# Retention's queries and keys through a DRAM scratch, two changed waiting rules and float32 norm sums in a two-layer hybrid encoder

## The chip, the cores and the metric

One core of a Trainium2 chip runs the whole program. The metric is the device time of one execution in microseconds (us). Engines are named as the profile names them: PE (TensorE matmuls), PEld (its weight loads), DVE (VectorE), ACT (ScalarE), POOL (GpSimd) and SP (SyncE), whose queue (SPq) issues nearly all of the transfers here.

## The reference

Two layers on a (1, 512, 1024) float32 input. What is computed in each:

```
x = x + 0.5 * SwiGLU(RMSNorm(x))                       # d_ff 2816
h = RMSNorm(x);  P = h @ W_in                          # A, B, C heads and three gates
A: 4 heads of differential attention: q, k of two maps each, normed and rotated,
   block-causal mask, softmax(s0) - lam * softmax(s1), values of 128, RMS norm per head
B: 8 heads of chunked attention, q and k normed, a relative-position bias, values of 64
C: 4 heads of retention: q and k rotated, scores times a decay, values of 128,
   RMS norm per head, times silu(g)
x = x + (sum_i sigmoid(g_i) * (branch_i @ W_branch_i)) @ W_out
x = x + 0.5 * SwiGLU(RMSNorm(x))
```

The kernel computes retention as one masked 512 x 512 product per head instead of a recurrence over chunks; the decay table holds zero above the diagonal.

## The kernel before

**Arithmetic.** Float32 accuracy is made of fp32r matmuls. Each operand is split into a high and a low part (ACT copies the high part, DVE subtracts: `xh`/`xl`, `wh`/`wl`, `yh`/`yl`, `qh`/`ql`), and a product takes three matmuls: high·high, high·low, low·high. Activations lie with features on the partitions, in tiles of 128 x 512 from a ring of 72 buffers (`big`). A weight tile of 128 x 1024 (`wr`) is loaded by SP into one of three raw buffers and split into `wh` and `wl`; 24 matmuls of 512 columns use one such tile in a projection.

**Stages of a layer.** An FFN, the mixer, an FFN. The mixer projects A's q, k, v, then B's, then the gates of branch 0 and C's gate `g` (four projections), multiplies A's result by its branch weights (`branch(0)`), projects C's q, k and v, then `branch(1)` for B and `branch(2)` for C. Each `branch` first computes eight gate projections from the normed input `xn` and then eight output tiles from the split results `ys` of that mixer, twelve matmuls each, `yh` and `yl` of four tiles.

**Heads between the projections.** Attention and retention run as side programs (Python generators), stepped between the matmuls of the projections. After every projection matmul `tick` may run the next piece of one of them. All instructions of an engine run in the order in which this planner emits them, so its order is fixed when the kernel is built. A small cost model (`Model`) keeps a clock per engine and a time for each tile; a piece is let in when PE's clock has passed the ready time of the tiles named in its last `yield` plus a margin: `then` none, `room` 800 ns, `product` 1600 ns, `turn` 2400 ns, and 1500 ns for the norm totals. A transfer counts as landed 2500 ns after its issue (`sent`). Two heads, one preparation and up to two finishing programs are active at a time.

**A head's end.** `settle_head` squares the head's output, splits the square and sums it over partitions with two matmuls against a matrix of ones (the total: `bank<-yh,ones`, then `bank<-yl,ones`). ACT copies half of the result to `ss`. When both heads of a pair are done, `finish` makes r = 1/sqrt on DVE (12 operations, `v`, `r`, `n`), SP scatters r to the two `rh` tiles with four transfers, and per head DVE multiplies `yu` by gain and `rh` (and for C by the gate `cs`), ACT makes `yh`, DVE `yl`.

**Stacked tiles.** The scores use tiles in which a head's 64 rows stand beside their other part, so that two matmuls do the work of three: for q the high over the low part, for k one tile of the high part twice and one of the low part twice (`qk`). [...] For A and B a tile takes two transfers of 64 rows (`twice`). For C the rows of a head come in two halves of 32 from two tiles (`rotated` gives rows 0 to 31 of all four heads in one tile and rows 32 to 63 in the other), so that a tile takes four transfers of 32 rows (L1003 to L1022). Per mixer these are 16 transfers for q and 32 for k, all on the SP queue, on which the weight loads stand too.

**The norm totals.** `norm_rows` sums the squares of x over the features. DVE or POOL adds the squares of the eight tiles into `acc`; then `acc` is split and summed with two fp32r matmuls against the ones. It serves the FFNs (L454, L479) and, through `norm_tokens`, the mixer.

The functions that the diff touches follow with their line numbers.

Of the kernel before, what the change touches and what calls it, by code (L numbers as in the profile page):

```python
# [11 lines left out]
F32 = mybir.dt.float32  # L12
# [7 lines left out]
S = 512  # L20
# [31 lines left out]
class Model:  # L52
# [29 lines left out]
        end, by = max(self.read.get(self.key(ap), [(0.0, "pe")]))  # L82
        self.slots[self.owner.pop(self.key(ap))] = end + self.LAG[by]

    def sent(self, ap, wait=2500):

        self.wrote[self.key(ap)] = max(self.t.values()) + wait, "pe"

# [34 lines left out]
def then(*aps):  # L123

    return aps, False, 0
# [7 lines left out]
def room(*aps):  # L133

    return aps, True, Kernel.MARGIN


def turn(*aps):

    return aps, True, Kernel.TURN  # L140


class Kernel:
# [254 lines left out]
            nc.scalar.activation(out=sq, in_=x, func=AF.Square)  # L398
            eng.tensor_tensor(out=self.acc, in0=self.acc, in1=sq, op=ALU.add)

    def norm_rows(self):

        parts = yield from self.split_side(self.acc)
        yield parts[1:], True, self.NORM
        b = self.bank()
        self.total(b, parts)
        self.rb = self.pool.tile([P, S], F32, tag="rb", bufs=2, name=self.name("rb"))
        yield then(b)
        yield from self.rsqrt_wide(self.rb, b, 1.0 / D, EPS)
# [40 lines left out]
    def opening_norm(self):  # L450
        for k in range(KD):
            self.norm_square(k, self.nc.vector)
            yield room(self.acc)
        yield from self.norm_rows()  # L454

    def ffn(self, l, gnext, late=1):
        nc = self.nc
        xs = self.xn
        ps = []

        def hidden():
            bg, bu = held.pop(0)
            t = self.big(F32, "t")
            nc.vector.tensor_tensor(out=t, in0=bg, in1=self.rb, op=ALU.mult)
            self.free(bg)
            nc.scalar.activation(out=t, in_=t, func=AF.Silu)
            nc.vector.tensor_tensor(out=t, in0=t, in1=bu, op=ALU.mult)
            self.free(bu)
            ps.append(self.split2(t, "p"))

        held = []
        for f in range(NF):
            if self.opening:
                held.append(self.open(xs))
                self.prio.append([0, self.opening_norm(), "n", None, True])
                continue
            bg = self.proj(xs)
            if f == 0:
                self.prio.append([0, self.norm_rows(), "n", None, True])  # L479
                self.step(self.prio)  # L480
            if f >= late:
                self.settle()
                if len(held) > 1:
                    hidden()
            held.append((bg, self.proj(xs)))
            if f >= late:
                hidden()
        while held:
            hidden()
        rb = self.rb  # L490
        self.xn = []
        wt = None
        at = 8
        for m in range(KD):
            b = self.bank()
            for f in range(NF):
                if at == 8:
                    wt, at = self.chunk(), 0
                c = slice(at * P, (at + 1) * P)
                at += 1  # L500
                self.mm3(b, (wt[0][:, c], wt[1][:, c]), ps[f], f == 0, f == NF - 1)
            t = self.big(F32, "t")
            cuts = (0, 256, S) if gnext is None and m == KD - 1 else (0, S)
            for c in (slice(i, j) for i, j in zip(cuts, cuts[1:])):
                nc.vector.scalar_tensor_tensor(out=t[:, c], in0=b[:, c], scalar=0.5, in1=rb[:, c], op0=ALU.mult, op1=ALU.mult)
                nc.vector.tensor_tensor(out=self.x[m][:, c], in0=self.x[m][:, c], in1=t[:, c], op=ALU.add)
                if gnext is None:
                    nc.sync.dma_start(out=self.a["out"][m][:, c], in_=self.x[m][:, c])
            self.free(b)
            if gnext is not None:  # L510
                self.norm_part(m, gnext)
            if gnext == C_MX:
                nc.sync.dma_start(out=self.xd[m], in_=self.x[m])
                if m == 1:
                    self.consts = self.layer_consts(l)
# [222 lines left out]
    def settle_head(self, o, st, h):  # L738

        nc = self.nc  # L740
        y, sq = self.big(F32, "yu"), self.big(F32, "sq")
        nc.scalar.activation(out=sq, in_=o, func=AF.Square)
        nc.scalar.activation(out=y, in_=o, func=AF.Copy)
        self.free(o)
        parts = yield from self.split_side(sq)
        yield room(parts[1])
        b = self.bank()
        self.total(b, parts)
        yield then(b)
        if st["rows"][h // 2] is None:  # L750
            st["rows"][h // 2] = self.big(F32, "ss")
        own = slice(64 * (h % 2), 64 * (h % 2) + 64)
        nc.scalar.activation(out=st["rows"][h // 2][own], in_=b[own], func=AF.Copy)
        self.free(b)
        st["yu"][h] = y
# [25 lines left out]
    def a_head(self, h, st):  # L781
        nc = self.nc
        es = self.weights()
        sums = {}

        def combine(i, e):
            s0, s1 = sums[i]
            for s in sums[i]:
                nc.vector.reciprocal(s, s)
            nc.vector.tensor_tensor(out=s1, in0=s1, in1=st["nlam"], op=ALU.mult)  # L790
            nc.vector.tensor_scalar(out=es[i], in0=es[i], scalar1=s0, scalar2=None, op0=ALU.mult)
            nc.vector.scalar_tensor_tensor(out=es[i], in0=e, scalar=s1, in1=es[i], op0=ALU.mult, op1=ALU.add)

        yield room(*(st[s][2 * h + c][0] for s in "qk" for c in range(2)))
        for i in range(NB + 1):
            if i < NB:
                bank = self.scores(st["q"][2 * h], st["k"][2 * h], i)
                yield then(bank)
                n = P * (i + 1)
                s = sums[i] = [self.small(1, "s") for _ in range(2)]  # L800
                self.softmax(bank, i, self.mask, s[0], es[i])
                yield room()
                bank = self.scores(st["q"][2 * h + 1], st["k"][2 * h + 1], i)
            if i:
                yield then(e)
                combine(i - 1, e)
            if i < NB:
                yield then(bank)
                e = self.big(F32, "e1")[:, 0:n]
                self.softmax(bank, i, self.mask, s[1], e)  # L810
                if i < NB - 1:
                    yield room()
        yield turn(*es)
        pt = yield from self.transposed(es)
        yield "av"
        o = yield from self.values(pt, st["v"], slice(h * P, (h + 1) * P))
        yield from self.settle_head(o, st, h)
        self.flags.add(f"A{h}")

    def b_head(self, h, st):  # L820
        nc = self.nc
        tb = self.table()
        es = self.weights()
        yield room(*(st[s][h][0] for s in "qk"))
        for i in range(NB):
            bank = self.scores(st["q"][h], st["k"][h], i)
            yield then(bank)
            s = self.small(1, "s")
# [14 lines left out]
        y, t = st["yu"][h // 2]  # L843
# [159 lines left out]
    def c_prep(self, halves, out, s):  # L1003


        parts = []
        for y in halves:
            parts.append((yield from self.split_side(y)))
        yield then(parts[1][1])
        for h in range(4):  # L1010
            hi, lo = ([p[i][32 * h:32 * h + 32] for p in parts] for i in range(2))
            a, b = h % 2 * 64, 64 - h % 2 * 64
            both = []
            for one, two in ((hi, hi), (lo, lo)) if s == "k" else ((hi, lo),):
                t = self.big(F32R, "qk")
                for at, pieces in ((a, one), (b, two)):
                    for i, x in enumerate(pieces):
                        self.nc.sync.dma_start(out=t[at + 32 * i:at + 32 * i + 32].bitcast(F32), in_=x.bitcast(F32))  # L1018
                self.model.sent(t)
                both.append(t)  # L1020
            out.append((both[0], both[-1]))
            self.flags.add(f"{s}C{h}")  # L1022
# [196 lines left out]
```

## Time and profile before

| what | us |
|---|---|
| median of 3 runs | 2547.62 |
| the three runs | 2541.91, 2547.62, 2548.82 |
| the profiled execution | 2555.1 |
| its span in the trace | 2553.3 |
| PE busy in the span | 2524.6 |
| mean granted TensorE clock | 0.997 |

How to read the rows: a timeline row gives the start in the span, the length, engine, line, operation, the tile written and the tiles read, the shape, and in brackets the engine's idle time just before it with what ended it. L48 is the line of a recording helper through which every PE, DVE, ACT and POOL instruction passes, so tiles tell the places apart. [...] An SPq row is the issue of a transfer; the landing times are in the page's section 6.

### The profile page before, as it was taken

The numbers are of one execution on the slowest core, as the hardware profiler recorded it, in microseconds if no ns is written. First come the engines' busy times: TensorE is split into PE (matmuls) and PEld (weight loads), VectorE is DVE, ScalarE is ACT, GpSimd is POOL, SyncE is SP. The second block draws the span as 40 slices with busy tenths as digits, with TensorE's granted clock in tenths as the row PEclk, the third lists the DMA queues.
The fourth block names the chain that finished last, engine by engine and source line by source line (L and its number), as shares of the span: only waits on it lengthen the run. The fifth ranks groups of instructions, "written<-read, shape, count | busy, mean of one in ns | idle before, by whom it ended". The sixth has DMA issues, their size and how long they took to land.

```text
span 2553.3 us, 28964 instructions
## 1 busy us (share of the span) xinstructions
PE 2524.6 (99%) x11226; PEld 2054.2 (80%) x11226; DVE 1376.2 (54%) x2180; ACT 920.2 (36%) x1397; POOL 140.3 (5%) x104
## 2 busy tenths in 40 slices
PE   9999999999999999999999999999989999999999
PEld 7888888887788888888888888888878888888887
DVE  6344337676867653443354343386778676543332
ACT  4233223553553333332223332245435533333321
POOL 0000001000102100000000001010001022000000
PEclk9999999999999999999999999999999999999999
DMA  4333334526432433333333333445274334333332
GB/s 165 93 93 97 109 118 130 141 83 169 129 118 75 141 98 99 95 95 99 92 98 91 97 89 117 127 118 139 84 181 121 112 85 136 98 97 99 91 111 71
DMA packets 96617, 280.91 MB, mean 110 GB/s; under 512 B 13536, under 2 KB 14944, under 8 KB 96480
## 3 DMA queue, kind: packets, MB, share of 16 engines
q1 hardware_dynamic: 95760, 278.45, 37.9%
q8 instruction: 88, 1.44, 0.2%
q10 hardware_dynamic: 720, 0.62, 0.1%
q14 instruction: 49, 0.40, 0.1%
HBM read 237.08 MB, written 6.29 MB: 95 GB/s over the span
## 4 chain that ended last, share of the span: by engine, by line
PE 87%; DVE 6%; DMA 2%; SPq 2%; issue 1%; ACT 1%; DVEq 0%; ACTq 0%
PE bank L48 87%; DVE wl L48 1%; SPq L667 1%; DVE n L48 1%; SPq L1018 1%; DVE e L48 1%; DVE g L48 1%; DVE r L48 1%; ACT wh L48 1%; DMA qk<-ql 0%; DMA qk<-qh 0%; DMA x<-in_xt 0%; DMA rh<-r 0%; DMA wr<-in_w 0%; DVE z L48 0%
## 5 line engine op out<-in xcount | busy, mean ns | idle before, releaser
L48 DVE TENSOR_TENSOR wl<-wr,wh 128x1024 fp32r<-128x1024 f32 x422 | 529.6, 1256 | 713.3 <-ACT wh L48 711.9
L48 PE MATMUL bank<-xh,wh 128*128 128x512 f32 x1920 | 759.2, 395 | 0.1
L48 PE MATMUL bank<-xl,wh 128*128 128x512 f32 x1920 | 757.9, 395 | 0.4 <-DVE xl L48 0.2
L48 PE MATMUL bank<-xh,wl 128*128 128x512 f32 x1920 | 757.8, 395 | 0.0
L48 ACT ACTIVATE wh<-wr 128x1024 fp32r<-128x1024 f32 x422 | 445.7, 1057 | 763.9 <-PE bank L48 664.3
L48 PEld LDWEIGHTS bank<-xh,wh 128*128 128x128 f32 x1920 | 361.7, 188 | 78.9 <-ACT xh L48 1.4
L48 PEld LDWEIGHTS bank<-xl,wh 128*128 128x128 f32 x1920 | 361.6, 188 | 78.7 <-DVE xl L48 1.8
L48 PEld LDWEIGHTS bank<-xh,wl 128*128 128x128 f32 x1920 | 361.5, 188 | 78.8
L48 PE MATMUL bank<-ph,wh 128*128 128x512 f32 x704 | 278.2, 395 | 0.0
L48 PE MATMUL bank<-pl,wh 128*128 128x512 f32 x704 | 277.5, 394 | 0.0
L48 PE MATMUL bank<-ph,wl 128*128 128x512 f32 x704 | 277.1, 394 | 0.0
L48 PE MATMUL bank<-wl,xh 128*128 128x512 f32 x448 | 178.9, 399 | 0.0
L48 PE MATMUL bank<-wh,xl 128*128 128x512 f32 x448 | 178.7, 399 | 0.0
L48 PE MATMUL bank<-wh,xh 128*128 128x512 f32 x448 | 178.3, 398 | 0.0
L48 PEld LDWEIGHTS bank<-ph,wl 128*128 128x128 f32 x704 | 132.6, 188 | 30.7
L48 PEld LDWEIGHTS bank<-ph,wh 128*128 128x128 f32 x704 | 132.7, 188 | 30.0
L48 PEld LDWEIGHTS bank<-pl,wh 128*128 128x128 f32 x704 | 132.7, 188 | 29.5
L48 ACT ACTIVATE e<-e,m 128x512 f32<-128x512 f32 (+3 forms) x128 | 71.7, 560 | 131.8 <-DVE m L48 127.3
L48 ACT ACTIVATE t<-t 128x512 f32<-128x512 f32 x88 | 55.6, 632 | 162.5 <-DVE t L48 162.5
L48 POOL TENSOR_TENSOR acc<-acc,sq 128x512 f32<-128x512 f32 x30 | 39.4, 1315 | 1117.2 <-PE bank L48 840.3
L48 PEld LDWEIGHTS bank<-wh,xl 128*128 128x128 f32 x448 | 84.4, 188 | 17.4
L48 PEld LDWEIGHTS bank<-wl,xh 128*128 128x128 f32 x448 | 84.3, 188 | 17.2
(145 smaller groups left out, 2489.7 us busy)
## 6 DMA issues: line engine op xcount, KB each, us to landing
wr<-in_w SPq DMA_DIRECT2D x422, 512.0 KB, 3.6
qk<-qh SPq DMA_DIRECT2D x96, 128.0 KB, 3.0
qk<-ql SPq DMA_DIRECT2D x96, 128.0 KB, 2.6
xd<-x SPq DMA_DIRECT2D x16, 256.0 KB, 2.8
tb<-in_tbias SPq DMA_DIRECT2D x16, 256.0 KB, 2.9
rh<-r SPq DMA_DIRECT2D x32, 128.0 KB, 5.0
x<-xd SPq DMA_DIRECT2D x16, 256.0 KB, 5.5
qk<-yh SPq DMA_DIRECT2D x48, 64.0 KB, 2.0
```

The source lines that it names most:

```text
L48: return call(*args, **kw)
L667: self.nc.sync.dma_start(out=t[o].bitcast(F32), in_=x.bitcast(F32))
L1018: self.nc.sync.dma_start(out=t[at + 32 * i:at + 32 * i + 32].bitcast(F32), in_=x.bitcast(F32))
```

## The change

Four edits.

1. `c_prep` no longer sends rows from SBUF to SBUF. It writes each of the four split parts of q (or k) to a DRAM tile of shape [head, part, 32, 512] with one transfer each, waits for the DRAM tile in the planner, and loads each stacked tile with one transfer of 128 partitions; for k the two halves of a tile read the same rows (`to_broadcast`). Per mixer that is 8 writes and 12 loads in place of 48 transfers.
2. The planner reckons 4000 ns instead of 2500 for a `sent` transfer (3000 for the DRAM tile). `a_head` and `b_head` wait, in the planner, for both tiles of each q and k and no longer for the first alone.
3. `settle_head` lets the total in with `turn` instead of `room`, for all heads of A and C.
4. The four norm totals of the FFNs become one float32 matmul each, on `acc` itself (`whole=True`); ACT's and DVE's split of `acc` goes there. The mixer's two stay as they were.

```diff
-    def sent(self, ap, wait=2500):
+    def sent(self, ap, wait=4000):
...
-    def norm_rows(self):
-
-        parts = yield from self.split_side(self.acc)
-        yield parts[1:], True, self.NORM
-        b = self.bank()
-        self.total(b, parts)
+    def norm_rows(self, whole=False):
+
+        if whole:
+            yield (self.acc,), True, self.NORM
+            b = self.bank()
+            self.nc.tensor.matmul(out=b, lhsT=self.ones.bitcast(F32), rhs=self.acc, start=True, stop=True)
+        else:
+            parts = yield from self.split_side(self.acc)
+            yield parts[1:], True, self.NORM
+            b = self.bank()
+            self.total(b, parts)
...
-        yield from self.norm_rows()
+        yield from self.norm_rows(whole=True)
...
-                self.prio.append([0, self.norm_rows(), "n", None, True])
+                self.prio.append([0, self.norm_rows(whole=True), "n", None, True])
...
         parts = yield from self.split_side(sq)
-        yield room(parts[1])
+        yield turn(parts[1])
...
-        yield room(*(st[s][2 * h + c][0] for s in "qk" for c in range(2)))
+        yield room(*(t for s in "qk" for c in range(2) for t in st[s][2 * h + c]))
...
-        yield room(*(st[s][h][0] for s in "qk"))
+        yield room(*(t for s in "qk" for t in st[s][h]))
...
     def c_prep(self, halves, out, s):
-        parts = []
-        for y in halves:
-            parts.append((yield from self.split_side(y)))
-        yield then(parts[1][1])
+        to = self.dram.tile([4, 4, 32, S], F32, tag=f"c{s}", bufs=1, name=self.name(f"c{s}"))
+        for i, y in enumerate(halves):
+            parts = yield from self.split_side(y)
+            yield then(parts[1])
+            for j, x in enumerate(parts):
+                self.nc.sync.dma_start(out=to[:, 2 * j + i], in_=x.bitcast(F32))
+        self.model.sent(to, 3000)
+        yield then(to)
         for h in range(4):
-            hi, lo = ([p[i][32 * h:32 * h + 32] for p in parts] for i in range(2))
-            a, b = h % 2 * 64, 64 - h % 2 * 64
             both = []
-            for one, two in ((hi, hi), (lo, lo)) if s == "k" else ((hi, lo),):
+            for c in (slice(0, 2), slice(2, 4)) if s == "k" else (slice(0, 4),):
+                src = to[h, c].rearrange("c r n -> (c r) n")
+                if s == "k":
+                    src = src[None].to_broadcast([2, 64, S])
                 t = self.big(F32R, "qk")
-                for at, pieces in ((a, one), (b, two)):
-                    for i, x in enumerate(pieces):
-                        self.nc.sync.dma_start(out=t[at + 32 * i:at + 32 * i + 32].bitcast(F32), in_=x.bitcast(F32))
+                self.nc.sync.dma_start(out=t.bitcast(F32), in_=src)
                 self.model.sent(t)
                 both.append(t)
             out.append((both[0], both[-1]))
```

Since the planner sets the order, the edits move pieces in both mixers. Three places follow.

PE, from the last total of C's heads to the first output tile of branch 2 in mixer 0, before. `bank<-yl,ones` ends the total of head 3; `yh_6588` and `yh_6637` are heads 0 and 1, `yh_6875` and `yh_6897` heads 2 and 3, whose r comes from that total:

```order
L48 MATMUL bank_6738<-yh_6701,ones 128x512
L48 MATMUL bank_6738<-yl_6702,ones 128x512
L48 MATMUL bank_6736<-xl_1846,wh_6627 128x512
...
L48 MATMUL bank_6943<-xh_2524,wl_6861 128x512
L48 MATMUL bank_6993<-yh_6588,wh_6904 128x512
...
L48 MATMUL bank_6993<-yh_6875,wh_6904 128x512
L48 MATMUL bank_6993<-yl_6876,wh_6904 128x512
...
L48 MATMUL bank_6993<-yh_6897,wh_6904 128x512
```

The same place now (`yh_6640`, `yh_6666`: heads 0 and 1; `yh_6930`, `yh_6936`: heads 2 and 3):

```order
L48 MATMUL bank_6851<-yh_6797,ones 128x512
L48 MATMUL bank_6851<-yl_6798,ones 128x512
L48 MATMUL bank_6841<-xh_2141,wh_6745 128x512
...
L48 MATMUL bank_6894<-xh_2519,wl_6803 128x512
L48 MATMUL bank_6962<-yh_6640,wh_6838 128x512
...
L48 MATMUL bank_6962<-yh_6930,wh_6838 128x512
L48 MATMUL bank_6962<-yl_6931,wh_6838 128x512
...
L48 MATMUL bank_6962<-yh_6936,wh_6838 128x512
```

Between the total and branch 2's first matmul stood 143 matmuls; now there are 39. The second mixer has the same numbers.

SP, around the four transfers of r for C's heads 2 and 3 in mixer 0 (`rh`, two of each), before:

```order
L200 DMA wr_6753<-in_w 128x1024
L200 DMA wr_6821<-in_w 128x1024
L769 DMA rh_6829<-r_6757 64x512 x2
L769 DMA rh_6832<-r_6757 64x512 x2
L200 DMA wr_6854<-in_w 128x1024
L200 DMA wr_6879<-in_w 128x1024
```

and now:

```order
L200 DMA wr_6821<-in_w 128x1024
L200 DMA wr_6858<-in_w 128x1024
L774 DMA rh_6922<-r_6863 64x512 x2
L774 DMA rh_6925<-r_6863 64x512 x2
L1061 DMA x_6940<-xd_88 128x512
L1061 DMA x_6941<-xd_89 128x512
```

What follows them is now the reload of x (eight transfers) instead of four weight loads; the `wr_6858` ahead of them waits for a buffer that DVE's `wl_6839` frees, which stands on DVE just before the first operation of this r.

PE at the start of branch 0 in mixer 0, where B's keys are transposed (`z` by `ident`) and B's first scores stand (`qk,qk`), before:

```order
L48 MATMUL bank_4803<-ident,z_3738 128x128
L48 MATMUL bank_4827<-yh_4121,wh_4662 128x512
...
L48 MATMUL bank_4827<-yh_4187,wl_4663 128x512
L48 MATMUL bank_4835<-ident,z_3697 128x128
...
L48 MATMUL bank_4827<-yh_4764,wh_4662 128x512
L48 MATMUL bank_4862<-qk_4780,qk_4499 128x256
L48 MATMUL bank_4862<-qk_4783,qk_4499 128x256
```

and now:

```order
L48 MATMUL bank_4762<-ident,z_3741 128x128
L48 MATMUL bank_4774<-yh_4080,wh_4641 128x512
...
L48 MATMUL bank_4774<-yl_4192,wh_4641 128x512
L48 MATMUL bank_4781<-ident,z_3696 128x128
...
L48 MATMUL bank_4839<-yh_4754,wl_4642 128x512
L48 MATMUL bank_4874<-qk_4786,qk_4565 128x256
L48 MATMUL bank_4874<-qk_4789,qk_4565 128x256
```

The four groups of transposes, three of which stood ahead of the branch, now stand apart; from the first of them to the first scores there are 24 other matmuls instead of 10. From the total of A's head 3, further up, to the matmul that reads that head's `yh` there are 112 instead of 124.

## The prediction

> **What bounds the kernel now.** I read the page first, then a table by stretch of the span, then what TensorE (PE) waits for. The page gives the span and the busy times:
>
> ```profile
> span 2553.3 us, 28964 instructions
> PE 2524.6 (99%) x11226; PEld 2054.2 (80%) x11226; DVE 1376.2 (54%) x2180; ACT 920.2 (36%) x1397; POOL 140.3 (5%) x104
> ```
>
> PE is the bound nearly everywhere, so an edit can only pay where PE stands still. The table by stretch (start and end, length, PE busy with its count, PEld, DVE, ACT, POOL, granted clock, DMA share, GB/s) says where that is:
>
> ```profile
> 580.00:643.00 63.00, 56.14 (x245) 44.46 (x244) 43.16 (x90) 23.40 (x43) 0.00 (x0) 0.92 0.73 180
> 1000.00:1688.00 688.00, 688.00 (x2976) 559.92 (x2975) 290.18 (x344) 204.18 (x243) 24.14 (x21) 1.00 0.34 100
> 1852.00:1912.00 60.00, 53.90 (x235) 42.31 (x234) 42.07 (x86) 21.34 (x39) 0.00 (x0) 0.94 0.73 180
> 2079.00:2549.00 470.00, 469.56 (x2054) 385.00 (x2052) 208.62 (x240) 138.85 (x168) 17.14 (x12) 1.00 0.34 101
> ...
> 618.20:628.50 10.30, 8.34 (x22) 6.42 (x23) 3.65 (x7) 1.60 (x4) 0.00 (x0) 0.50 0.91 203
> ```
>
> From 1000 to 1688 us (end of one mixer, two FFNs) and from 2079 to the end PE never stops: 688/2976 = 0.231 us per matmul of 512 columns, the price used below. The losses lie in the two mixers, the worst near 580–643 and 1852–1912, and there the granted clock drops: 10.3 us at 0.50 in the last row. The table of PE's waits (total, times, longest) names the releasers:
>
> ```profile
> PE bank L48 <- DMA qk<-ql: 4.9, 5, 1.4
> PE bank L48 <- DVE m L48: 3.6, 4, 1.3
> PE bank L48 <- DVE yl L48: 3.6, 4, 1.4
> PE bank L48 <- DVE e L48: 3.5, 2, 2.2
> PE bank L48 <- DMA qk<-qh: 1.7, 3, 0.7
> PE bank L48 <- ACT yh L48: 1.3, 2, 0.6
> PE bank L48 <- DVE z L48: 1.1, 2, 0.7
> PE bank L48 <- ACT pt L48: 1.0, 2, 0.7
> PE bank L48 <- DVE vl L48: 0.9, 2, 0.7
> ```
>
> That is 21.6 us in all. The timeline places single waits of both mixers (in brackets: idle before, releaser):
>
> ```profile
> 460.46 0.36 PE L48 MATMUL bank<-qk,qk 128*128 128x256 f32 x1 [0.71 <-DMA qk<-ql]
> 1730.73 0.36 PE L48 MATMUL bank<-qk,qk 128*128 128x256 f32 x1 [0.85 <-DMA qk<-ql]
> 553.92 0.73 PE L48 MATMUL bank<-qk,qk 128*128 128x512 f32 x2 [0.82 <-DVE m L48]
> 1824.49 0.73 PE L48 MATMUL bank<-qk,qk 128*128 128x512 f32 x2 [0.81 <-DVE m L48]
> 806.78 0.39 PE L48 MATMUL bank<-yh,ones 128*128 128x512 f32 x1
> 808.46 0.51 PE L48 MATMUL bank<-yl,ones 128*128 128x512 f32 x1 [1.29 <-DVE yl L48]
> 2078.70 0.50 PE L48 MATMUL bank<-yl,ones 128*128 128x512 f32 x1 [1.40 <-DVE yl L48]
> ```
>
> **What the change takes away.** Four kinds of wait lose their cause.
>
> *First scores of A* (0.71 + 0.85). The heads now ask for both tiles and reckon 4000 ns for a transfer. In the new order 7 matmuls instead of 2 stand between kA's last transposes and these scores, 5 × 0.231 = 1.2 us more. Gain 1.6 us.
>
> *Banks held by DVE's m* at 553.92 and 1824.49. DVE was sitting on A's first yu until rh landed; in the new order that yu stands further behind its rh. Gain 1.6 us.
>
> *vl and pt* (0.9 + 1.0 in the waits). They follow C's transfers, behind which the weight loads (wr) stood on the SP queue:
>
> ```profile
> 694.77 2.42 SPq L1018 DMA_DIRECT2D qk<-yh  x4
> ...
> 712.66 2.48 SPq L1018 DMA_DIRECT2D qk<-yl  x4
> 715.19 0.58 SPq L890 DMA_DIRECT2D tb<-in_tbias  x1
> 715.87 0.39 SPq L200 DMA_DIRECT2D wr<-in_w  x1
> ```
>
> 32 issues at about 0.6 us hold wr for 21 us. Now it is 20 issues per mixer instead of 48, the longest block without a wr being the 8 loads of k: 8 × 0.6 plus a wait for the writes to land, under 9 us. Gain 1.9 us.
>
> *The total of a C head* (1.29 + 1.40). turn asks for 2400 ns after yl instead of 800. Gain 2.7 us.
>
> These rows sum to 7.8 us idle. A stall costs slightly more than its idle row: 806.78 to 808.46 is 1.68 us where 0.23 is normal, 1.45 against the 1.29 shown. Ten stalls of 0.16 more make **−9.4 us**.
>
> **What it adds: four norm totals in float32.** Each replaces two fp32r matmuls (2 × 0.23 = 0.46 us) by one float32 matmul of 512 columns. Bounds come from two places:
>
> ```profile
> 1.49 5.49 PE L48 MATMUL bank<-warm 128*128 128x512 f32 x6 [1.49 <-DVE warm L48]
> ...
> 810.31 0.38 PE L48 MATMUL bank<-pt,v 128*128 128x128 f32 x2
> 810.45 0.48 PE L48 MATMUL bank<-xl,wh 128*128 128x512 f32 x1
> 810.77 0.40 PE L48 MATMUL bank<-xh,wl 128*128 128x512 f32 x1
> ```
>
> The 3 warm matmuls (6 hardware instructions) take 5.49/3 = 1.83 us each, in the opening microseconds. The float32 values of 128 columns at full clock: from 810.31 to 810.77 are 0.46 us, in which one matmul of 0.23 starts too, so 0.23 per 128 columns, 0.92 for 512. I take 0.92, from the running kernel: 4 × 0.46 = **+1.8 us** (upper end 4 × 1.37 = 5.5). The ACT and DVE split that goes was covered by PE's other matmuls.
>
> **What it adds: a wait ahead of branch 2.** The later admission of heads and the longer gap before each total push C's last heads back. The new order has 39 matmuls between the last total (yl,ones) and branch 2's first matmul, and 45 until the first that reads head 2's yh; before, 143 and 149. All of the path from that total to yh must fit under them. In the profile of before it ran like this (mixer 0: DVE, ACT, SP, and the landing times of section 6):
>
> ```profile
> 816.27 0.40 PE L48 MATMUL bank<-yl,ones 128*128 128x512 f32 x1
> ...
> 818.34 0.59 ACT L48 ACTIVATE ss<-bank 64x512 f32<-64x512 f32 x1
> ...
> 819.49 0.42 DVE L48 TENSOR_SCALAR v<-ss 128x512 f32<-128x512 f32 x1
> 826.94 0.43 DVE L48 TENSOR_SCALAR r<-r 128x512 f32<-128x512 f32 x1
> 836.78 0.75 DVE L48 SCALAR_TENSOR_TENSOR yu<-yu,cols,rh 128x512 f32<-128x512 f32 x1 [3.12 <-DMA rh<-r]
> 837.57 0.69 DVE L48 TENSOR_TENSOR yu<-yu,cs 128x512 f32<-128x512 f32 x1
> ...
> 838.29 0.63 ACT L48 ACTIVATE yh<-yu 128x512 fp32r<-128x512 f32 x1 [3.02 <-DVE yu L48]
> ...
> 831.25 2.43 SPq L769 DMA_DIRECT2D rh<-r  x4
> ...
> qk<-ql SPq DMA_DIRECT2D x96, 128.0 KB, 2.6
> ...
> rh<-r SPq DMA_DIRECT2D x32, 128.0 KB, 5.0
> ...
> qk<-yh SPq DMA_DIRECT2D x48, 64.0 KB, 2.0
> ```
>
> From the start of yl,ones: matmul 0.40, ss 0.59, start of v at about 1.2 (the 818.34 here stood behind a weight copy); v to r 7.9 (819.49 to 827.37): 9.1. Then rh. From its first issue to yu were 5.5 us (831.25 to 836.78), with a wr issued just ahead on the queue. In the new order the wr ahead of it waits only for a copy that DVE makes before v, so it has long landed. The price therefore lies between 2.6 (2.0 for qk<-yh and one more issue of 0.6) and 5.5; I take 3.4: qk<-ql, of the same size as rh, lands in 2.6, one more issue is 0.6, and a hop 0.2. yu at 12.6, its second product, then yh: 838.29 + 0.63 − 836.78 = 2.1, so **14.7**. PE's 45 matmuls end at 10.6. Idle 4.1. Then head 2's yl (0.69), head 3's yu (0.75 + 0.69), yh (0.63) and yl (0.69) follow in series on DVE and ACT, 3.6 with hops, to 18.4, where an unhindered PE would read head 3's yl at 11.5. **Loss 6.9 us per mixer** (6.1 at 2.6, 9.0 at 5.5).
>
> And the clock: about 4 us of idle within 12 us gave 10.3 us at 0.50 at 618. Half clock for 6 to 10 us, partly inside the wait, costs 0 to 5 us; I take 3. The second mixer has the same order there. Sum **2 × 9.9 = +19.8 us**, from 12.2 to 28. [...]
>
> **What it moves, at nothing: branch 0 and B's first scores.** Of the waits above, ql 3.3, m 2.0, yl 0.9, e 3.5, qh 1.7, yh 1.3 and z 1.1 lie here, 13.8 us in both mixers, plus half clock: (1 − 0.92) × 63 + (1 − 0.94) × 60 = 8.6 by the table. In the new order A's last total has 112 instead of 124 matmuls ahead of the branch matmul that reads its head (2.8 us less cover), and B's first scores stand 24 instead of 10 matmuls behind kB's first transposes (3.2 us more). DVE's e still reuses ring tiles that SP's queued copies of kB read. One side gives what the other takes: **0**, between −22 (13.8 + 8.6, all gone) and +8 (2.8 later per mixer, a longer half clock).
>
> C's round trip through DRAM I cost at nothing: its loads come more than three weight tiles (24 matmuls, 5.5 us each) ahead of C's first scores. Without that cover it would cost two landings, 2.0 us at least each.
>
> **Sum.** 2555.1 (profiled execution; span 2553.3 and 1.8 around it) − 9.4 + 1.8 + 19.8 + 0 = 2567.3. The profiled execution is 7.5 above the median of 2547.62, so **2560** as a median.
>
> **Rivals.**
>
> *No change.* rh lands in 2.6 and the clock holds: 2 × 6.1 = 12.2 instead of 19.8, 2552. For: no wr in front. Against: over 4 us of idle.
>
> *Faster.* B's scores, with 3.2 us more cover, no longer stop PE, and the chain of late e's and half clock with them: −22 instead of 0, 2538. It decides as soon as more than about 20 of these 22 us go. For: their waits start with the qk transfers, 1.39 us at most. Against: the shorter cover of A's chain, and the ring tiles.
>
> *Worse.* rh at its usual 5.0 and one issue more, and a longer half clock: 28 instead of 19.8, with branch 0 worse by 8: 2576.
>
> *C's writes and reads block wr.* SP waits for the landing ahead of the loads; if weights ran out for 5 us per mixer, 2570. Against: three raw and three split weight tiles in hand, 33 us. [...]
>
> **Chances.** Forecast 0.53, no change 0.22, faster 0.12, worse 0.09, wr 0.04. About 0.3% (7.6 us) can be told from no change: faster 0.12, same 0.22, slower 0.66. The range, 2545 to 2574, takes in the no-change case and half of the worse one.
>
> **What would show it.** Right: in the new profile PE waits for ACT yh and DVE yl of C just ahead of branch 2, 4 us or more at once, with a granted clock near 0.5 behind it, in both mixers; no waits of the first scores of A, on m at 553, on vl, or on yl,ones. Float32 totals 0.9 us apart. Wrong: if branch 2 starts without a stop of 4 us, or if the stretch around branch 0 keeps clock 1.00.

## The result

The change makes the kernel slower by 86 us, seven times what was predicted.

| what | us |
|---|---|
| before, median of 4 runs beside it | 2545.07 |
| changed, median of 4 runs | 2631.3 (2628.35 to 2632.97) |
| ratio of the two | 1.0342, 95% interval 1.0326 to 1.0359 |
| predicted | 2560 (2545 to 2574) |
| profiled execution of the changed kernel, its span | 2632.86, 2630.8 |

The ratios leave out three disturbed executions, one each of e3, e6 and the kernel before, that took hundreds of microseconds or more longer than the rest.

The page of the changed kernel has the same work on PE in a longer span:

```profile
span 2630.8 us, 28838 instructions
PE 2523.2 (96%) x11226; PEld 2059.5 (78%) x11226; DVE 1367.5 (52%) x2176; ACT 918.7 (35%) x1393; POOL 139.0 (5%) x104
```

PE is busy for 2523.2 us instead of 2524.6, so the whole difference of the two spans is time in which PE stands still: 107.6 us now, 28.7 before. (The lower clock, 0.980 on the mean against 0.997, lengthens the busy time of the changed kernel too; the kernel before had slower FFNs in its profile, 12.4 us by "The sum" below, and the two about cancel.) The table of PE's waits says for whom PE stands:

```profile
PE bank L48 <- ACT pt L48: 67.5, 2, 34.2
PE bank L48 <- DVE m L48: 13.0, 4, 4.8
PE bank L48 <- ACT yh L48: 8.7, 4, 3.6
PE bank L48 <- DVE z L48: 6.0, 8, 2.2
PE bank L48 <- DVE e L48: 4.0, 2, 2.0
...
PE bank L48 <- DMA qk<-ql: 1.2, 2, 0.6
```

Two waits of 34 us, one in each mixer, are new and alone hold 67.5 us. The prediction has no such wait. Waits that it did take away are gone: qk<-ql fell from 4.9 to 1.2 us, vl is absent, and yl (3.6 before) is down to 0.2.

The timeline of the changed kernel shows what the first long wait stands on (PE, ACT, then SP's queue; the last line is from the table of what SP waits for):

```profile
759.50 0.80 PE L48 MATMUL bank<-pt,vv 128*128 128x128 f32 x2 [34.20 <-ACT pt L48]
...
758.22 1.06 ACT L48 ACTIVATE wh<-wr 128x1024 fp32r<-128x1024 f32 x1 [35.67 <-DMA wr<-in_w]
759.18 0.64 ACT L48 ACTIVATE pt<-bank 128x128 f32<-128x128 f32 x2
...
693.87 1.76 SPq L1026 DMA_DIRECT2D qk<-cq  x4
696.87 0.79 SPq L200 DMA_DIRECT2D wr<-in_w  x1
...
710.29 30.57 SPq L1026 DMA_DIRECT2D qk<-ck  x8
740.97 4.99 SPq L200 DMA_DIRECT2D wr<-in_w  x1
...
SPq L1026 <- DMA ck<-yh: 19.0, 2, 10.1
```

PE waits for ACT's pt. ACT had nothing to compute with: its next instruction in order, the copy wh of a weight, stood 35.67 us for the load wr, and pt stands behind it. That wr was issued at 740.97 and was ready at 758.2, 17 us later, where the median before was 3.6. Ahead of it on SP's queue are the eight loads of C's k tiles. SP first waited 10.1 us for the writes of k to land. Issuing the eight then took 30.57 us, 3.8 us each on average, while the four loads of q, with just as many bytes each, took 1.76, 0.44 us each. Between two weight loads on the queue thus lie 44 us (696.87 to 740.97). The table by stretch shows what the DMA engines did meanwhile (the last two columns are their busy share and GB/s):

```profile
710.00:741.00 31.00, 15.29 (x77) 12.19 (x75) 8.29 (x15) 6.29 (x11) 0.00 (x0) 0.81 0.14 54
741.00:760.00 19.00, 0.51 (x3) 0.51 (x3) 0.69 (x1) 1.60 (x3) 0.00 (x0) 0.50 0.48 142
760.00:770.00 10.00, 10.00 (x44) 8.08 (x43) 5.67 (x12) 4.56 (x9) 0.00 (x0) 0.82 0.26 75
```

As an estimate from the share, 0.14 is a little over two of 16 engines (2/16 = 0.125) at full load, moving 54 GB/s, where the same queue moved 164 GB/s from 676 to 693 us and 210 from 693 to 698. PE stood from 725.3 to 759.5, and not for lack of split weights: counted from the start of the trace, 116 weight tiles were split by then and PE had used 114.6 of them. It is the order that stopped it, since its next instruction is the product with the pt that stands behind the late wh on ACT. After that it ran 10 us at a mean clock of 0.82, 1.8 us lost.

### The profile page after: what moved, and what is told of

It reads as the page before. It is cut to its first block, busy times and chain, and to the rows that moved or that the text cites. A ratio compares the mean times of both kernels' runs of the same rounds, so it can differ in the third digit from the quotient of the medians.

```text
span 2630.8 us, 28838 instructions
## 1 busy us (share of the span) xinstructions
PE 2523.2 (96%) x11226; PEld 2059.5 (78%) x11226; DVE 1367.5 (52%) x2176; ACT 918.7 (35%) x1393; POOL 139.0 (5%) x104
## 4 chain that ended last, share of the span: by engine, by line
PE 90%; DMA 3%; DVE 3%; SPq 3%; ACT 1%; issue 1%; DVEq 0%; ACTq 0%
PE bank L48 90%; DMA wr<-in_w 1%; SPq L1026 1%; SPq L672 1%; DMA qk<-ql 1%; DMA qk<-qh 1%; DVE n L48 1%; DVE z L48 0%; DVE e L48 0%; DVE wl L48 0%; DVE r L48 0%; ACT wh L48 0%; DMA x<-in_xt 0%; DVE yu L48 0%; DVE g L48 0%
## 5 line engine op out<-in xcount | busy, mean ns | idle before, releaser
L48 PE MATMUL bank<-yh,wh 128*128 128x512 f32 x192 | 81.8, 426 | 21.7 <-DVE m L48 13.0
L48 PEld LDWEIGHTS bank<-wh,xh 128*128 128x128 f32 x448 | 84.3, 188 | 17.6
```

Source lines behind the costliest of these rows:

```text
L48: return call(*args, **kw)
```

## The experiments

Four theories stood against each other. SHAPE: the source of a k load, two readings of the same 64 rows (`[2, 64, 512]`), keeps only about two of 16 DMA engines busy (the share of 0.14). ROUND TRIP: a store to DRAM and a reload are slow whatever the shape. ORDER: the heads that run later starve PE. REREAD: reading the same rows twice in one transfer is slow.

### e1: k tiles loaded in two transfers

```diff
                 src = to[h, c].rearrange("c r n -> (c r) n")
-                if s == "k":
-                    src = src[None].to_broadcast([2, 64, S])
                 t = self.big(F32R, "qk")
-                self.nc.sync.dma_start(out=t.bitcast(F32), in_=src)
+                for at in (0, 64) if s == "k" else (0,):
+                    self.nc.sync.dma_start(out=t[at:at + src.shape[0]].bitcast(F32), in_=src)
```

> The changed kernel, only each of C's k tiles is loaded from the scratch by two transfers of 64 partitions instead of one whose source has an outer dimension of 2 (all compute engines keep the order of the changed kernel). Theory SHAPE (the loads of k keep only 2 of the 16 DMA engines busy: DMA share 0.14 and 51 GB/s while they run; the next weight stands behind them and PE stops for 34 us): those stops go, 2 x (34 + 2 of half clock) = 72 us less, about 2559 us, and no PE wait over 6 us. Rival ROUND TRIP (storing to DRAM and reading back is slow whatever the shape): within 10 us of 2631. Rival ORDER (the heads that run later starve PE): 2631.

Measured: 2563.31 us, against 2547.99 for the kernel before beside it (ratio 1.0057, 1.0036 to 1.0078). The order of the compute engines is that of the changed kernel, the bytes read are the same, and 68 us are gone. SP's queue, and the table by stretch while the loads are issued:

```profile
705.57 11.80 SPq L1025 DMA_DIRECT2D qk<-ck  x16
717.47 0.53 SPq L200 DMA_DIRECT2D wr<-in_w  x1
...
706.00:718.00 12.00, 12.00 (x61) 9.75 (x60) 7.33 (x15) 5.70 (x11) 0.00 (x0) 1.00 0.57 173
```

Twice as many transfers are issued in 11.8 us instead of 30.57, at 173 GB/s instead of 54. This speaks for SHAPE, and against ORDER and ROUND TRIP as causes of the long stop. It does not yet tell the shape from the double reading of one transfer.

### e2 and e3: the scratch in the old order

e2 is the kernel before with nothing but the new `c_prep`; e3 has the two transfers of e1 in it as well.

> The kernel before with nothing but the changed c_prep (scratch, one load per stacked tile, k with the outer dimension of 2). SHAPE: the 34 us stops are there in the old order too, about 2547 + 72 - 3 = 2616 us (2600 to 2630). ROUND TRIP: the same, 2616. ORDER: no stop, 2540 to 2550.

> The kernel before with the scratch, and k loaded in two transfers of 64 partitions. SHAPE: no long stop, and the waits on vl and pt after C's old transfers are gone: 2547 - 3 = 2544 us (2538 to 2550). ROUND TRIP: about 2616. ORDER: 2544.

Measured: e2 2609.14 us (ratio 1.0244, 1.0217 to 1.027), e3 2547.85 (ratio 0.9997, 0.9981 to 1.0014). The long stop comes with `c_prep` alone, and goes with the shape of the load. In e2, too, the eight issues are one block:

```profile
705.79 30.14 SPq L1021 DMA_DIRECT2D qk<-ck  x8
736.03 4.99 SPq L890 DMA_DIRECT2D tb<-in_decay  x1
741.12 2.59 SPq L200 DMA_DIRECT2D wr<-in_w  x3
...
PE bank L48 <- DVE m L48: 56.0, 6, 26.1
```

PE waited 26 us at most instead of 34: the late weight lands 4.4 us earlier there (its copy starts at 753.8 instead of 758.2), and PE comes one weight tile further in its order before it meets a piece that waits. The releaser's name differs, the cause does not: DVE's m stands behind wl, and wl behind the late wh.

e3 lies within its range (2538 to 2550) but 4 us above its point, and is no faster than before. The scratch did not save the 1.9 us of vl and pt waits: PE waits 3.3 us for pt there instead of 1.0. SP waits up to 8.1 us for the writes of k to land, then issues 16 loads in one block of 12.16 us, so that no weight load is issued for about 26 us (694.1 to 719.9), no less than the 21 us of the old transfers. While only such writes are under way, the changed kernel moves 100 GB/s at a DMA share of 0.26 (705 to 710 us), by estimate about 4 of 16 engines. The target of a write is `[4, 32, 512]`; no run changes that shape, so whether the outer 4 is the reason is not shown.

### e4: an outer dimension of two without reading anything twice

k as in e1; the scratch is padded, so that the two 64-row blocks of a q tile lie apart and q's single load has a source of `[2, 64, 512]` that reads each row once.

```diff
-        to = self.dram.tile([4, 4, 32, S], ...)
+        to = self.dram.tile([4, 2, 3, 32, S], ...)
...
+                    src = to[h, c, 0:2].rearrange("c i r n -> c (i r) n")
+                    self.nc.sync.dma_start(out=t.bitcast(F32), in_=src)
```

> As e1 (k in two transfers of 64 partitions), but the scratch is padded so that q's one load per tile reads two blocks of 64 rows that lie apart: a source with an outer dimension of 2 and no row read twice. SHAPE (the outer dimension, not the reading of the same rows twice): q's 4 loads take 4 x 256 KB / 51 GB/s = 20 us on 2 engines, and the weight behind them is late: 10 to 30 us slower than e1, DMA share near 0.14 while they run. Rival REREAD (reading the same DRAM rows twice in one transfer is what is slow): the time of e1.

Measured: 2602.55 us (ratio 1.0209, 1.0187 to 1.0231), 39 us above e1, more than the 30 that were the upper end. While q's loads run:

```profile
691.00:711.00 20.00, 19.71 (x89) 15.87 (x87) 8.21 (x25) 6.12 (x16) 0.00 (x0) 1.00 0.15 55
```

0.15 of the engines and 55 GB/s, with no row read twice. REREAD falls: it is the outer dimension of two. At 55 GB/s the four loads are 19 us, near the expected 20. That it cost more comes from what stands behind: the writes of k follow q on the queue and are late as well. ACT waited 15.7 us for one of them (`ck<-yh`) before it could write vh, DVE's vl follows vh, and PE stops 8.4 us on vl, then 2.7 on e and some more.

### e9: half the dose

Heads 0 and 1 with the one transfer, heads 2 and 3 with two.

> The changed kernel with the one-transfer load of k for heads 0 and 1 (4 of the 8 loads) and two transfers of 64 partitions for heads 2 and 3. SHAPE, with one queue in order: the 8 loads took 41 us and stopped PE 34, so 7 us are slack; 4 loads of 5.1 and 8 issues of 0.7 are 26 us, a stop of about 19 in each mixer: e1 + 2 x (19 + 2 - 2) = about 2600 us, stops on pt of 15 to 22 us. A rival by which the broadcast costs once and not per load (a first read of fresh rows): 2630 or 2563.

Measured: 2594.94 us (ratio 1.0202, 1.0183 to 1.022). The stops on pt are 16.4 us and less, where full dose made 34.2 and e1 made 2.2 at most: half the loads, half the stop. The rival's two times, 2630 and 2563, are both missed: the cost is paid per load.

### e5 and e6: what else is in the changed order

e1 is 15 us above the kernel before, where the prediction had put the change. Two edits take parts of the new order back: e5 is e1 with `room` ahead of a head's total, e6 is e1 with `sent(wait=2500)`.

> e1 with room (800 ns) again instead of turn ahead of the total of a head. By the order 95 matmuls instead of 39 then stand between C's last total and branch 2. Theory BRANCH 2 (the last finish of C has too little cover in the changed order: PE idle 3.7 and 1.5 and two shorter stops ahead of branch 2 in e1, and half clock behind them): these go in both mixers, 2 x (6 + 2) = 16 us, and the waits of yl,ones return, 2 x 1.4: e1 - 13, about 2550 us. Rival BRANCH 0 (the excess over the kernel before sits at branch 0, with PE idle 11.3 of 63 us there in e1 and 6.9 before): within 4 us of e1's 2563.

> e1 with 2500 ns instead of 4000 for a transfer in the planner; 111 matmuls between C's last total and branch 2. BRANCH 2: the stop ahead of branch 2 goes (16 us), the total's wait stays gone: about 2546 us. BRANCH 0: a gain only if the idle time between 580 and 643 us falls from 11.3 to about 7 us (2 x 4).

Measured: e5 2546.74 us (ratio 1.0005, 0.9995 to 1.0015), e6 2542.84 (ratio 0.9984, 0.9975 to 0.9994). e1 to e5 is 16.6 us and e1 to e6 20.5; the stop ahead of branch 2 is what both shorten. e6 has none, and BRANCH 0 falls there: between 580 and 643 us PE is idle for 10.0 us, not the 7 that this rival asked for. Of the 18.0 us between the profiles of e1 and e6, branch 2 holds 17.3 when counted as under "The sum" below; of the 13.0 us between e1 and e5 it holds 6.7, the rest lying mostly at C (4.6, the waits on pt are gone) and branch 0 (2.7). In e5 part of the stop stays although 95 matmuls, 22 us, now lie over a chain of 14.4:

```profile
818.03 0.40 PE L48 MATMUL bank<-yl,ones 128*128 128x512 f32 x1
842.14 0.50 PE L48 MATMUL bank<-yh,wh 128*128 128x512 f32 x1 [0.58 <-ACT yh L48]
844.91 0.55 PE L48 MATMUL bank<-yh,wh 128*128 128x512 f32 x1 [1.31 <-ACT yh L48]
...
828.78 0.43 DVE L48 TENSOR_SCALAR r<-r 128x512 f32<-128x512 f32 x1
838.51 0.75 DVE L48 SCALAR_TENSOR_TENSOR yu<-yu,cols,rh 128x512 f32<-128x512 f32 x1 [0.23 <-DMA rh<-r]
...
815.29 17.74 SPq L200 DMA_DIRECT2D wr<-in_w  x3
833.14 2.39 SPq L774 DMA_DIRECT2D rh<-r  x4
```

r was done at 829.2, but rh was issued at 833.14: a weight load that waits for a buffer stood ahead of it on SP's queue. With the landing behind that weight it took 9.3 us from r to yu; in the changed kernel, with nothing that waits in front, it took 3.0. In e6 another stop grew instead: z of B's keys holds PE for 6.0 us in mixer 0 and 6.7 in mixer 1, because DVE sat on A's yu:

```profile
603.89 0.75 DVE L48 SCALAR_TENSOR_TENSOR yu<-yu,sub,rh 128x512 f32<-128x512 f32 x1 [4.54 <-DMA rh<-r]
610.67 1.89 DVE L48 TENSOR_TENSOR z<-z,y 128x512 f32<-128x512 f32 x3
...
611.41 3.13 PE L48 MATMUL bank<-ident,z 128*128 128x128 f32 x8 [6.02 <-DVE z L48]
```

So both stops have one thing in common: rh shares a queue with transfers that wait.

### e10, e11 and e12: rh on another queue

e10 is e6 with the four rh transfers issued by POOL; in e11 the second transfer of every stacked tile of A and B goes there as well; e12 is the kernel before with rh on POOL and nothing else.

```diff
-                nc.sync.dma_start(out=rs[-1][64 * half:64 * half + 64], in_=r[...])
+                nc.gpsimd.dma_start(out=rs[-1][64 * half:64 * half + 64], in_=r[...])
```

> e6 (k in halves, 2500 ns) with the rh transfers on POOL's queue instead of SP's. Theory QUEUE (rh is late since it stands on SP's queue among the qk and wr transfers; DVE waited 4.5 us for it at 599 to 604 in e6, and z of B's keys behind it stopped PE for 6.2 and 6.8 us): that wait shrinks below 2 us, z's stop below 3 us, and some half clock with it: 2542.8 - 2 x 5 = about 2533 us, 2526 to 2538. Rival LANDING (it is late for its landing, which is no shorter on POOL's queue): 2540 to 2546.

> e10 with the second of the two transfers of each stacked tile of A and B on POOL's queue too. If SP's issues at 0.6 us each (24 in a row for B's keys, 14 us) hold B's first scores and the ring tiles that DVE's e reuses (stops of 1.2 and 2.1 us per mixer and half clock behind them): 2533 - 2 x 4 = about 2525 us. If a transfer issued by POOL costs more than 0.6 us or lands later: at or above e10.

> The kernel before with nothing but the rh transfers on POOL's queue. If that queue alone makes e10's gain: DVE's 13.2 us of waits for rh, the banks held by m (1.8) and most of the stops at branch 0 with their half clock go, about 2545 - 12 = 2533 us (2528 to 2538). If e10 needed the scratch, turn and the norm totals as well: 2538 to 2546.

Measured: e10 2528.93 us (ratio 0.9942, 0.9929 to 0.9956), e11 2549.5 (1.002, 1.001 to 1.0029), e12 2541.95 (0.9992, 0.9979 to 1.0006). e10 is the fastest of all and beats both kernels. The answer for its rh tiles, and its wait for z:

```profile
DMA to landing us min/median/max: 2.2/3.0/5.8
...
605.98 0.33 PE L48 MATMUL bank<-ident,z 128*128 128x128 f32 x1 [1.41 <-DVE z L48]
```

rh lands in a median of 3.0 us (5.0 in the kernel before; no median is on record for e6), and the stop at z shrinks from 6.02 to 1.41 us. QUEUE and LANDING are not fully told apart by that: the landing itself became shorter too. e11 shows the queue's part: when POOL's queue is filled with qk transfers, rh stands behind those, DVE waits 4.47 us for it again, and the gain is gone, and more. e12's expectation missed: DVE's 13.2 us of waits for rh are gone there too, and rh lands in 2.7 us, but in the kernel before, where other things hold branch 0 as well (PE still waits 5.6 us for qk<-ql and 4.8 for yl), that gives nothing that the interval separates from zero. e10 needs the other edits, and which of them it needs was not tried.

### e7: the float32 totals alone, and e8: k's rows written twice

> The kernel before with nothing but the four float32 norm totals. If a float32 matmul of 512 columns takes 0.92 us: 4 x 0.46 = +1.8 us, ratio 1.0007; if 1.83 us: +5.5, ratio 1.0022.

Measured: 2542.06 us, ratio 0.9987 (0.9978 to 0.9996): a gain of about 0.1%, and neither of the two losses. The total itself costs what was forecast (changed kernel, PE):

```profile
2268.51 1.02 PE L48 MATMUL bank<-acc,ones 128*128 128x512 f32 x2
2268.97 0.79 PE L48 MATMUL bank<-xl,wh 128*128 128x512 f32 x1
2269.60 0.39 PE L48 MATMUL bank<-xh,wl 128*128 128x512 f32 x1
```

From 2268.51 to 2269.60 are 1.09 us, less 0.23 for the matmul between: 0.86. A possible source of the gain stands under the last heading.

e8 gives each k tile one load of 128 rows that lie together, by writing k's rows to the scratch twice; it also has `turn`, on the kernel before.

> [...] SHAPE: each k load is issued in about 0.45 us as q's are (1.76 for four), no wait of PE on pt behind it, no wait of yl,ones: 2547.6 - 3 - 3 = about 2541 us, ratio 0.997 to 0.999. If writing the rows twice costs: 2548 or more.

Measured: 2554.46 us (ratio 1.0037, 1.0023 to 1.0051), slower. Eight writes of 256 KB stand in front of the loads, the engines are half in use (0.51 at 172 GB/s from 694 to 726 us), and PE waits 12.3 us on pt in six stops. The stop of 6.0 us on z in each mixer is the one known from e6, so that not all of the loss belongs to the writing:

```profile
717.13 8.29 SPq L1020 DMA_DIRECT2D qk<-ck  x8
...
PE bank L48 <- DVE pt L48: 12.3, 6, 3.3
PE bank L48 <- DVE z L48: 11.7, 2, 6.0
```

The expectation that its k loads would be issued at 0.45 us each was wrong: 1.04, behind the writes.

## Why the prediction was wrong

The direction held, the size did not, and one step holds most of the difference.

**The step that failed: "C's round trip through DRAM I cost at nothing".** I counted its transfers and their issue time at 0.6 us each ("8 × 0.6 plus a wait for the writes to land, under 9 us") and never asked how many DMA engines a load with a source of `[2, 64, 512]` would use. Measured, the block without a weight load is 44 us: some 10 us of waiting for the writes, 30.6 us of issue at 54 GB/s, and then a weight that took 17 us to land: 2 × (34 + 2) = 72 us by the profile, 68 us by e1 against the changed kernel. The rival "C's writes and reads block wr" had the mechanism, the late weights, with 5 us per mixer and a chance of 0.04. The cover set against it, three raw and three split tiles or 33 us, was near the mark: at the last weight load before the block PE had 5.5 tiles ahead of it. But from that load to the landing of the next one lay 61 us (696.87 to 758.2), and PE stopped after 28 of them, with 1.4 tiles unused, since ACT's pt stands behind the late copy.

How many engines such a load keeps busy, the runs answer as a share of the 16: 0.14 (changed kernel) and 0.15 (e4) while loads with a source of `[2, 64, 512]` run, 0.57 (e1) while loads of 64 plain rows do. Sixteen times the share, that is by estimate 2.2 to 2.4 engines and about 9; no view shows the engines one by one, and why the shape counts is not shown. The round trip as such does not account for the loss: SP does wait for the writes to land, but e1 and e3 wait much the same (up to 9.2 and 8.1 us), and e3, with the round trip and k in two loads of 64 rows, equals the kernel before.

**Right in mechanism, with a size a little off: the wait ahead of branch 2.** Predicted, from yl,ones: v at 1.2, r done at 9.1, yu at 12.6, yh at 14.7, idle 4.1. In the changed kernel:

```profile
871.74 0.40 PE L48 MATMUL bank<-yl,ones 128*128 128x512 f32 x1
...
873.12 0.42 DVE L48 TENSOR_SCALAR v<-ss 128x512 f32<-128x512 f32 x1
880.57 0.43 DVE L48 TENSOR_SCALAR r<-r 128x512 f32<-128x512 f32 x1
883.99 0.75 DVE L48 SCALAR_TENSOR_TENSOR yu<-yu,cols,rh 128x512 f32<-128x512 f32 x1 [1.79 <-DMA rh<-r]
...
886.18 0.52 PE L48 MATMUL bank<-yh,wh 128*128 128x512 f32 x1 [3.56 <-ACT yh L48]
888.96 0.80 PE L48 MATMUL bank<-yh,wh 128*128 128x512 f32 x1 [0.83 <-ACT yh L48]
...
880.00:890.00 10.00, 5.41 (x17) 3.09 (x16) 6.72 (x11) 4.30 (x6) 0.00 (x0) 0.83 0.72 222
890.00:900.00 10.00, 10.00 (x38) 8.02 (x38) 7.22 (x8) 2.33 (x3) 3.72 (x3) 0.83 0.51 153
```

v at 1.4, r at 9.3, yu at 12.3, yh at 14.4, idle 3.6. Idle in the stretch 4.6, and (1 − 0.83) × 20 = 3.4 of half clock: 8.0 us per mixer against 9.9 predicted. By the sign that I had set, a stop of 4 us or more at once, it falls just short (3.56 and 3.50). e6, which takes the late order back, has no such stop. From the first issue of rh to yu are 3.0 us (881.03 to 883.99), against the 3.4 taken; no row shows the hop of 0.2 in it. One reading of mine was too generous: I took 3 us of half clock from the 10.3 us at 0.50 in the profile of before and put them down to about 4 us of idle. In the 50 us ahead of that stretch PE had no single stop longer than 0.64 us, and in the last 12.2 of them it stood 2.0 us in all (606 to 618.2, 10.23 busy). What lowers the clock, no run varied.

**Right: the waits taken away.** First scores of A, m at 553 and 1824, and the total of a C head are gone: the changed kernel's PE has no stop between 10 and 602 us, none at the second mixer's A and none at yl,ones. **Wrong among them:** vl and pt were to save 1.9 us; e3 shows no saving.

**Wrong in size: branch 0 "at nothing".** The stretch 560 to 660 us holds it in mixer 0; the changed kernel, with DVE's wait for the ring tiles:

```profile
560.00:660.00 100.00, 88.04 (x393) 70.69 (x392) 63.20 (x130) 36.05 (x65) 2.56 (x2) 0.93 0.57 142
...
DVE e L48 <- DMA qk<-qh: 31.5, 4, 10.3
```

and the kernel before:

```profile
560.00:660.00 100.00, 93.14 (x432) 74.96 (x431) 73.51 (x152) 42.93 (x80) 3.52 (x2) 0.95 0.60 153
```

5.1 us more idle and 2 more of half clock; the second mixer has the same, so some 14 us against the 0 I took and the 8 of my upper end. The cover that B's first scores gained is real (qk<-ql 1.2 us in the table of waits), but PE only meets the next wait: m, 4.85 us at once, as DVE waits up to 10.3 us to write e into ring tiles that the queued copies of kB still read. I had named those tiles and given them no price. In e1 the same stretch has 88.74 us busy, so nearly the same idle time, but clock 0.98, about 1 us more than before in all; the rest of the difference between e1 and the changed kernel here is the clock. That e1 comes out at 2563, close to the forecast of 2560, is thus in part luck: its stops at branch 0 and the pace of the FFNs, told below, were not in the sum.

**Right as a price, wrong as an effect: the float32 totals.** 0.86 us each against 0.92, yet e7 does not lose.

**The sum.** From the start of each matmul to the next, beyond the usual distance of its shape (0.23 us for 512 columns, though such a row is 0.395 us long on average), added up by stage over both mixers, the changed profile differs from the one before by: C's late weights +68.0 us, branch 2 +16.5, branch 0 +13.4, the waits taken away −7.9, the FFNs −12.4, the rest +0.3: 77.9 of the 77.8 us between the two profiled executions. The FFNs' part is not work that was saved: two of the four in the profile of before ran at a lower pace, told under the last heading.

## What to carry to other kernels

Before costing a transfer by its count and bytes, look at the outermost dimension of its source (these runs did not vary the target's): one transfer with an outer dimension of 2 took about 5 us (256 KB at 54 GB/s), where two plain ones took 1.5 (11.8 us for eight pairs). The bill comes from what is queued behind it: the next weight load was issued 44 us after the one before it, took 17 us to land instead of 3.6, and PE paid 34 us per mixer. And a small transfer on a chain that PE waits for (rh here) is worth a queue on which nothing stands that waits for a buffer, once the rest of the order lets it count: 13.9 us from e6 to e10, nothing sure from the kernel before to e12.

## What the runs showed of the hardware

**Issuing can take long.** Of the eight loads of k in mixer 0 the first three were issued in 0.5 to 0.6 us each, the other five in 5.1 to 6.3 us each, about the time in which 256 KB move at 54 GB/s (4.9 us); the loads of q, of the same size but with 128 rows as the outermost dimension, took 0.44 us each. What stands behind is held as well: in e4 the write behind q's loads took 7.13 us to issue, in e1 0.53. The time to issue a transfer is thus not a constant: in the changed kernel the loads of q and k, 256 KB each, took from 0.33 to 7.2 us.

**fp32r matmuls have two paces.** Long stretches of an FFN run at either 200/876 = 0.2283 or 200/859 = 0.2328 us per matmul, with clock 1.00 and no wait in both. In the profile of before (the first two rows) the stretch 100 to 300 us is at the slow pace and 1000 to 1200 at the fast one; e7 has the fast one at 100 to 300 (third row):

```profile
100.00:300.00 200.00, 200.00 (x859) 162.01 (x858) 77.85 (x91) 60.01 (x72) 4.59 (x6) 1.00 0.33 97
1000.00:1200.00 200.00, 200.00 (x876) 164.09 (x875) 80.79 (x91) 60.56 (x72) 1.34 (x1) 1.00 0.33 96
```

```profile
100.00:300.00 200.00, 200.00 (x876) 164.09 (x875) 80.38 (x94) 61.76 (x74) 4.59 (x6) 1.00 0.34 101
```

An FFN of some 1600 such matmuls is 7 us longer at the slow pace. In the five profiles of kernels with the fp32r pair as norm total 3 of 20 FFNs ran at it, two of them in the profile of before, which fits that this execution stood 7.5 us above the median; in the nine profiles with float32 totals none of 36 did. That fits e7's gain, and that e7's twelve runs lie within 5 us (2540.87 to 2545.77) while those of before beside them spread from 2539 to 2549. What sets the pace was not tried; that the float32 matmul has to do with it is only a guess.
